# A list schedule of its own for the second layer's attention

## The chip, the cores and the metric

The kernel runs on one core of a Trainium2 chip. The metric is the device time of one execution in microseconds, the median over several runs. TensorE (PE in the profile; PEld is its loading of stationary operands) multiplies matrices and transposes; VectorE is DVE, ScalarE is ACT, GpSimd is POOL, and SyncE (SP) issues the DMA transfers. Each engine works through its own queue in order; semaphores between the queues make an instruction wait for another engine's.

## What is computed

A trunk of two layers over 512 tokens of width 1024. Layer 0 mixes tokens with a recurrence and a long convolution; layer 1 with 2-D neighbourhood attention, 16 heads of 64. Each layer has a gated feed-forward block and a gated per-layer input behind its mixer. All in float32. The part that the change touches:

```python
for i in range(DEPTH):
    ...
    else:
        z = rmsnorm(h, na_norm[j]) @ na_w_qkv[j]
        h = h + neighbourhood_attention(z, na_q_g[j], na_k_g[j], na_rpb[j]) @ na_w_out[j]
    h = h + conv_ffn(h, ffn_norm[i], ffn_w_up[i], ffn_conv_w[i], ffn_conv_b[i], ffn_w_down[i])
    h = h + per_layer_embedding(h, p[i], ple_norm[i], ple_w_gate[i], ple_w_proj[i])

def neighbourhood_attention(z, q_g, k_g, rpb):
    q = split(rmsnorm(z[..., :D].reshape(B, L, H, dh), q_g) * (dh ** -0.5))
    k = split(rmsnorm(z[..., D:2 * D].reshape(B, L, H, dh), k_g))
    v = split(z[..., 2 * D:])
    ...
    # per token: 8 rows x 16 columns of neighbours, scores plus a position bias, softmax, values
```

## The kernel before

The mixer of layer 0 is recorded into a `Plan`, a list scheduler: each instruction becomes a step with an estimated price, a group and the steps it depends on; a group has a priority; `schedule()` picks, engine by engine, the step of the highest rank among those that could start now or within AHEAD microseconds, and stays with one form of matmul until a run of RUN microseconds is full. `write()` (L590) then issues the steps in the order found, and `in_order` has the framework keep it. The price of a VectorE or ScalarE instruction is a formula: 0.15 or 0.16 us and a little over or under 1 ns for each element of a row.

Everything behind it (feed-forward 0, input 0, the attention `mixer1`, feed-forward 1, input 1) is written straight, and the framework orders it by the code and its dependencies. `mixer1` does this:

- The norm. For each of 8 blocks of the hidden state h, ScalarE scales and casts a high part xh and VectorE makes the low part xl; ScalarE squares (nsq) and GpSimd adds the squares up (nacc). `sums` multiplies nacc by a column of ones, four matmuls of 128x1, to get the sums over partitions; `rsqrt` makes rstd of them on VectorE (rv) and GpSimd.
- The projections. `gemm_tok` makes one of q, k, v for half of the heads: 4 chunks of weights, each two of the 8 blocks deep, come by DMA into wraw and are split into whi (cast on ScalarE) and wlo (VectorE), three slots each. A chunk feeds 24 matmuls of 128x512 (xh by whi, xh by wlo, xl by whi for 4 blocks of tokens), one PSUM bank "g" for each block of tokens. `evac` scales a bank by rstd on ScalarE; q and k then get a norm of their own (sq, ss, rs). The results of `sums` are therefore needed first when the first bank of q is complete. For v, six DMAs make a copy vb that is shifted by 64 tokens.
- `attend`, for each of 8 head pairs: q and k are transposed on TensorE (L1843) into PSUM "m" and split into qh, ql, kh, kl; four score tiles "s" of 6 matmuls each (64 rows of the array, one head) are made; VectorE adds the bias table and takes the maximum, ScalarE the exponential (sc), VectorE the division; the probabilities are transposed (L1892) and copied to pt on ScalarE (L1894); 32 small matmuls a pair multiply va or vb by pt into PSUM "m"; the result is split into oh (ScalarE, L641) and ol (VectorE, L633).
- The out projection: `gemm` with oh and ol, two halves of the depth by two groups of columns, added into h.

The code goes: projections of the first four pairs, their attention, projections of the other four, their attention, out projection. On TensorE the framework lets matmuls of a later gemm fill gaps between attention's steps, bank by bank as `gemm_tok` writes them. PSUM has four banks "g", two "s" and two "m". `sums` is called behind the second chunk of the first gemm (kc == 2).

The matmul helper is L627, elementwise VectorE and GpSimd operations of two tensors L633, ScalarE's functions L636, casts L641.

Of the kernel before, what the change touches and what calls it, by code (L numbers as in the profile page):

```python
# [22 lines left out]
KT = D // P  # L23
# [569 lines left out]
class Kern:  # L593
# [1131 lines left out]
    def gemm_tok(self, wname, g, xs, evac, then=None):  # L1725

        K, groups = WEIGHTS[wname]
        ps = [self.pg.tile([P, S], F32, name="g") for _ in range(4)]
        for kc in range(0, KT, 2):
            off = (g * KT + kc) * P * S  # L1730
            hi, lo = self.load_split(self.a[wname][off:off + 2 * P * S].rearrange("(p a) -> p a", p=P), 1024)
            for t in range(4):
                for kk in range(2):
                    c = slice(kk * S, (kk + 1) * S)
                    xh, xl = [x[:, t * P:(t + 1) * P] for x in xs(kc + kk)]
                    last = kc + kk == KT - 1
                    self.mm(ps[t], xh, hi[:, c], kc + kk == 0, False)
                    self.mm(ps[t], xh, lo[:, c], False, False)
                    self.mm(ps[t], xl, hi[:, c], False, last)
                if kc == KT - 2:  # L1740
                    evac(t, ps[t])
            if then is not None and kc == 2:
                then()

    def mixer1(self):

        nc, a = self.nc, self.a
        ident = self.cst("ident")
        by_col = lambda t: t.rearrange("p (r c) -> p c r", c=64)
        col = lambda t: t.rearrange("p (c r) -> p c r", r=8)  # L1750
        with ExitStack() as st:
            pa = self.pool(st, "pa", side="right")
            po = self.pool(st, "po", side="left")
            pss = self.pool(st, "pss", bufs=2, space=PSUM)
            xs, acc = [], None
            for k in range(KT):
                xh = self.px.tile([P, S], F32R, name=f"xh{k}")
                xl = self.px.tile([P, S], F32R, name=f"xl{k}")
                self.split(col(xh), col(xl), by_col(self.h[k]), scale=self.par("na_norm", k))
                xs.append((xh, xl))  # L1760
            for k in range(KT):
                sq = self.pn.tile([P, S], F32, name="nsq", bufs=2)
                self.act(col(sq), by_col(self.h[k]), AF.Square)
                if acc is None:
                    acc = sq
                else:
                    new = self.pn.tile([P, S], F32, name="nacc", bufs=2)
                    self.tt(new, acc, sq, ALU.add, nc.gpsimd)
                    acc = new
            rstd = pa.tile([P, 4], F32, name="rstd")  # L1770

            def sums():
                ps = self.pm.tile([P, 4], F32, name="m")
                for t in range(4):
                    self.mm(ps[:, t:t + 1], acc[:, t * P:(t + 1) * P], self.cst("one"))
                self.rsqrt(rstd, ps, 1.0 / D, EPS)

            oh = [(po.tile([P, S], F32R, name=f"oh{k}"), po.tile([P, S], F32R, name=f"ol{k}")) for k in range(KT)]
            for half in range(2):
                qk, vv = self.qkv(pa, half, lambda k: xs[k], rstd, sums if half == 0 else None)  # L1780
                for m in range(half * 4, half * 4 + 4):
                    self.attend(pa, pss, m, qk, vv, oh[m])
            for k0 in (0, 4):
                for g in range(2):
                    def evac(j, ps, g=g):
                        t = self.h[g * 4 + j]
                        self.tt(t, ps, t, ALU.add)
                    self.gemm("na_w_out", g, k0, k0 + 4, lambda k: oh[k], evac)
            for k in range(KT):
                self.dump(f"a_{k}", self.h[k])  # L1790

    def rsqrt(self, out, src, scale, eps):

# [2 lines left out]
        self.nc.vector.tensor_scalar(out=v[:, :n], in0=src, scalar1=scale, scalar2=eps, op0=ALU.mult, op1=ALU.add)  # L1796
        self.tt(out, v[:, :n], self.epsc[:, 4:4 + n], ALU.pow, self.nc.gpsimd)

    def qkv(self, pa, half, xs, rstd, then):


        nc = self.nc
        qk = [[pa.tile([P, S], F32, name=f"{n}{t}") for t in range(4)] for n in "qk"]
        va = pa.tile([P, 4, S], F32, name="va")
        vb = pa.tile([P, 3, S], F32, name="vb")

        def evac(t, ps, x):
            sc = rstd[:, t:t + 1]
            if x == 2:
                self.act(va[:, t], ps, AF.Copy, scale=sc)  # L1810
                return
            z = qk[x][t]
            self.act(z, ps, AF.Copy, scale=sc)
            sq = pa.tile([P, S], F32, name="sq", bufs=1)
            self.act(sq, z, AF.Square)
            ss = pa.tile([P, 8], F32, name="ss", bufs=2)
            nc.vector.tensor_reduce(out=ss, in_=sq.rearrange("p (h d) -> p h d", d=64), axis=AX.X, op=ALU.add)
            r = pa.tile([P, 8], F32, name="rs", bufs=2)
            self.rsqrt(r, ss, 1.0 / 64, EPS)
            zv = z.rearrange("p (h d) -> p h d", d=64)  # L1820
            self.tt(zv, zv, r.unsqueeze(2).to_broadcast([P, 8, 64]), ALU.mult)

        for x in range(3):
            self.gemm_tok("na_w_qkv", half * 3 + x, xs, lambda t, ps, x=x: evac(t, ps, x), then if x == 0 else None)
        for t in range(3):
            nc.sync.dma_start(out=vb[0:64, t], in_=va[64:128, t])
            nc.sync.dma_start(out=vb[64:128, t], in_=va[0:64, t + 1])
        return qk, (va, vb)
# [4 lines left out]
    def attend(self, pa, pss, m, qk, vv, o):  # L1833

        nc, ident = self.nc, self.cst("ident")
        c0 = m % 4 * P
        tab = pa.tile([P, 3, 512], F32, name="tab", bufs=2)
        nc.sync.dma_start(out=tab, in_=self.a["rpb"][m].rearrange("p (b x) -> p b x", b=3))
        q, k = [], []
        for x, dst in enumerate((q, k)):  # L1840
            ps = self.pm.tile([P, S], F32, name="m")
# [7 lines left out]
        scs = {}  # L1849
        for bp in range(2):  # L1850
            for hd in range(2):
                rows = slice(hd * 64, hd * 64 + 64)
                ps = pss.tile([P, 2, 256], F32, name="s")
                for bi in range(2):
                    b = bp * 2 + bi
                    w0 = self.WIN[b][0]
                    self.mm3(ps[:, bi], q[0][rows, b * P:(b + 1) * P], q[1][rows, b * P:(b + 1) * P],
                             k[0][rows, w0:w0 + 256], k[1][rows, w0:w0 + 256], True, True)
                sc = scs[bp, hd] = pa.tile([P, 2, 256], F32, name="sc", bufs=4)
                mx = pa.tile([P, 2], F32, name="mx", bufs=3)  # L1860
                sm = pa.tile([P, 2], F32, name="sm", bufs=3)
                for bi in range(2):
                    tb = tab[:, self.WIN[bp * 2 + bi][3], hd * 256:hd * 256 + 256]
                    nc.vector.tensor_tensor_reduce(out=sc[:, bi], in0=ps[:, bi], in1=tb, op0=ALU.add,
                                                   op1=ALU.max, scale=1.0, scalar=-3e38,
                                                   accum_out=mx[:, bi:bi + 1])
                nc.vector.tensor_scalar(out=mx, in0=mx, scalar1=-1.0, scalar2=None, op0=ALU.mult)
                for bi in range(2):
                    self.act(sc[:, bi], sc[:, bi], AF.Exp, bias=mx[:, bi:bi + 1],
                             accum_out=sm[:, bi:bi + 1])  # L1870
                nc.vector.reciprocal(out=sm, in_=sm)
                for bi in range(2):
                    nc.vector.tensor_scalar(out=sc[:, bi], in0=sc[:, bi], scalar1=sm[:, bi:bi + 1],
                                            scalar2=None, op0=ALU.mult)
        pts = {}
        pso = self.pm.tile([P, 4, P], F32, name="m")

# [69 lines left out]
```

## Time and profile before

| | us |
|---|---|
| runs | 1593.35, 1597.08, 1598.9 |
| median | 1597.08 |
| profiled execution, its own time | 1602.47 |
| span of its trace, first to last instruction | 1600.7 |
| PE busy | 1531.0 (96%) |
| DVE busy | 973.9 (61%) |
| ACT busy | 718.8 (45%) |
| POOL busy | 341.0 (21%) |

The mean granted clock of TensorE over the span is 0.974 of full speed. Matmuls are pipelined: one that is shown with 0.39 us starts about 0.23 us behind the one ahead, so the time that a row of matmuls takes is read from start to start. "Idle before" in brackets is how long the engine stood before the row's first instruction and what released it. The stage that is changed begins near 924 us and ends near 1189 us.

### The profile page before, as it was taken

To read this page: it belongs to the slowest core of one execution; us is meant where nothing else is said; L and a number is where in the kernel's file an instruction comes from. 1 tells how busy PE (TensorE), PEld (TensorE's weight loads), DVE (VectorE), ACT (ScalarE), POOL (GpSimd) and SP (SyncE) were. 2 spreads that over 40 slices of the span, in tenths; PEclk is the share of its full clock that TensorE was granted. 3 is DMA by queue.
4 is the path that set the end of the run, shared out by engine and by line. 5 is a ranking of instruction groups with operands and counts; after the bars stand their busy time and mean duration, and the time that the engine had idled before them with its cause. 6 is when DMAs were issued, how large, how long until landed. Compare 5 with 4: busy or idle time off the path is not lost.

```text
span 1600.7 us, 24569 instructions
## 1 busy us (share of the span) xinstructions
PE 1531.0 (96%) x9520; PEld 1219.6 (76%) x9520; DVE 973.9 (61%) x1618; ACT 718.8 (45%) x1210; POOL 341.0 (21%) x296
## 2 busy tenths in 40 slices
PE   7999999979797999999999999999999999999998
PEld 6766777657585888888888878777678888888886
DVE  4875677775654477534674664565666665366655
ACT  5636455535344344313443554564554443144332
POOL 4654554433554000000001332011030000000020
PEclk9999999979898999999999999999999999999999
DMA  7456464766354323223243234224122332222431
GB/s 235 122 126 193 139 195 130 226 206 203 128 184 135 100 96 102 92 96 102 92 128 122 86 112 124 94 81 130 61 66 79 105 105 93 93 88 97 160 104 66
DMA packets 114583, 195.97 MB, mean 122 GB/s; under 512 B 27537, under 2 KB 57105, under 8 KB 114466
## 3 DMA queue, kind: packets, MB, share of 16 engines
q1 hardware_dynamic: 114466, 194.40, 38.4%
q8 instruction: 75, 1.23, 0.3%
q14 instruction: 42, 0.34, 0.1%
HBM read 163.95 MB, written 28.84 MB: 120 GB/s over the span
## 4 chain that ended last, share of the span: by engine, by line
PE 84%; DVE 5%; DMA 4%; ACT 3%; SPq 2%; issue 1%; POOL 1%; POOLq 0%; DVEq 0%; ACTq 0%
PE g L627 61%; PE b L590 19%; DVE w L590 3%; SPq L590 2%; PE m L627 2%; PE s L627 1%; ACT w L590 1%; PE m L1892 1%; DMA wr<-in_mix_w_in 1%; POOL w L590 1%; DMA wr<-in_dft_f 0%; POOL nacc L633 0%; ACT oh L641 0%; DVE u L633 0%; DVE uv L590 0%
## 5 line engine op out<-in xcount | busy, mean ns | idle before, releaser
L633 DVE TENSOR_TENSOR wlo<-wraw,whi 128x1024 fp32r<-128x1024 f32 x180 | 227.8, 1267 | 322.5 <-ACT whi L641 317.7
L641 ACT CAST whi<-wraw 128x1024 fp32r<-128x1024 f32 x180 | 188.2, 1046 | 406.7 <-PE g L627 398.5
L627 PE MATMUL g<-xh,whi 128*128 128x512 f32 x832 | 326.8, 393 | 8.9 <-ACT whi L641 8.9
L627 PE MATMUL g<-xh,wlo 128*128 128x512 f32 x832 | 325.3, 391 | 1.0 <-DVE wlo L633 1.0
L627 PE MATMUL g<-xl,whi 128*128 128x512 f32 x832 | 324.9, 391 | 0.0
L627 PEld LDWEIGHTS g<-xh,whi 128*128 128x128 f32 x832 | 157.0, 189 | 43.0 <-ACT whi L641 9.3
L627 PEld LDWEIGHTS g<-xh,wlo 128*128 128x128 f32 x832 | 156.8, 188 | 34.7 <-DVE wlo L633 1.7
L627 PEld LDWEIGHTS g<-xl,whi 128*128 128x128 f32 x832 | 157.1, 189 | 32.3
L633 POOL TENSOR_TENSOR nacc<-nsq 128x512 f32<-128x512 f32 x5 | 8.8, 1767 | 760.5 <-PE g L627 639.6
L590 PE MATMUL b<-xh,wp 128*128 128x512 f32 x432 | 151.0, 423 | 10.5 <-ACT wp L590 10.2
L627 PE MATMUL g<-hh,whi 128*128 128x512 f32 x352 | 137.2, 390 | 0.0
L627 PE MATMUL g<-hl,whi 128*128 128x512 f32 x352 | 137.0, 389 | 0.0
L627 PE MATMUL g<-hh,wlo 128*128 128x512 f32 x352 | 136.9, 389 | 0.0
L630 DVE SCALAR_TENSOR_TENSOR c<-u,prm,c 128x511 f32<-128x511 f32 x176 | 126.3, 746 | 6.4 <-ACT c L636 5.9
L590 PEld LDWEIGHTS b<-xh,wp 128*128 128x128 f32 x432 | 83.2, 197 | 36.2 <-ACT wp L590 12.0
L636 ACT ACTIVATE c<-u,prm 128x512 f32<-128x512 f32 x88 | 70.3, 816 | 70.7 <-DVE u L633 70.7
L590 POOL TENSOR_TENSOR wp<-wr,wp 128x512 fp32r<-128x512 f32 x62 | 82.5, 1343 | 50.0 <-ACT wp L590 41.0
L590 POOL TENSOR_TENSOR w<-w 128x256 f32<-128x256 f32 (+2 forms) x69 | 75.7, 1115 | 74.2 <-ACT w L590 57.1
L590 PE MATMUL b<-xl,wp 128*128 128x512 f32 x216 | 89.0, 418 | 0.0
L633 DVE TENSOR_TENSOR u<-g,rstd 128x512 f32<-128x512 f32 x104 | 71.3, 686 | 11.6 <-PE g L627 10.8
L627 PE MATMUL g<-wlo,xh 128*128 128x512 f32 x192 | 77.2, 402 | 0.0
L627 PE MATMUL g<-whi,xh 128*128 128x512 f32 x192 | 77.1, 401 | 0.0
(181 smaller groups left out, 2601.4 us busy)
## 6 DMA issues: line engine op xcount, KB each, us to landing
wraw<-in_up SPq DMA_DIRECT2D x88, 512.0 KB, 3.5
wraw<-in_down SPq DMA_DIRECT2D x44, 512.0 KB, 3.5
wr<-in_mix_w_in SPq DMA_DIRECT2D x52, 256.0 KB, 3.7
wraw<-in_na_w_qkv SPq DMA_DIRECT2D x24, 512.0 KB, 3.5
x<-ch_d SPq DMA_DIRECT2D x16, 640.0 KB, 5.1
ch_d<-w SPq DMA_DIRECT2D x64, 128.0 KB, 2.3
wraw<-in_gate SPq DMA_DIRECT2D x16, 512.0 KB, 3.5
tab<-in_rpb SPq DMA_DIRECT2D x8, 768.0 KB, 4.2
```

The lines of the kernel that those rows point to most:

```text
L590: getattr(e, method)(*args, **kw)
L627: return self.nc.tensor.matmul(out, lhsT, rhs, start=start, stop=stop, skip_group_check=not group)
L630: return self.nc.vector.scalar_tensor_tensor(out=out, in0=in0, scalar=scalar, in1=in1, op0=op0, op1=op1)
L633: return (eng or self.nc.vector).tensor_tensor(out=out, in0=in0, in1=in1, op=op)
L636: return self.nc.scalar.activation(out=out, in_=in_, func=func, **kw)
L641: self.nc.scalar.copy(h, src)
L1892: nc.tensor.transpose(pst[:, i], sc[:, i // 2, (i % 2) * P:(i % 2 + 1) * P], ident)
```

## The change

The body of `mixer1` behind the norm's splits is recorded into a `Plan` of its own, with AHEAD 0.2 and RUN 1.5, and without the rule by which layer 0's plan prices a cold clock. Groups: the sums ("rms"), each projection gemm, and for each head pair its transposes of q and k, each score tile and its values; a table ORDER1 gives the priorities. The gemms are chained one behind the other, values of a pair behind those of the pair before, and the out projection's four gemms are at the end of the chain. The sums are called behind the third chunk (kc == 4) and not behind the second. What is computed, and by which instructions, is the same.

```diff
@@ gemm_tok
-            if then is not None and kc == 2:
-                then()
+            if then is not None and kc == 4:
+                self.nc.behind["rms"] = self.nc.group
+                self.part("rms", then)
@@ mixer1
+            start = len(nc.cur_bb.bb.instructions)
+            real, self.nc = nc, Plan(nc)
+            nc = plan = self.nc
+            plan.AHEAD, plan.RUN, plan.DRAG = self.ATTEND
+            plan.cold = False
...
+            dense = []
+
+            def gemm(group, what, *args):
+
+                if dense:
+                    plan.behind[group] = dense[-1]
+                dense.append(group)
+                self.part(group, what, *args)
...
-                qk, vv = self.qkv(pa, half, lambda k: xs[k], rstd, sums if half == 0 else None)
+                qk, vv = self.qkv(pa, half, lambda k: xs[k], rstd, gemm, sums if half == 0 else None)
...
-                    self.gemm("na_w_out", g, k0, k0 + 4, lambda k: oh[k], evac)
+                    gemm(("out", k0, g), self.gemm, "na_w_out", g, k0, k0 + 4, lambda k: oh[k], evac)
+            self.nc = real
+            plan.bias = {g: 1000.0 * self.order1(g) for g in plan.firsts}
+            plan.write(plan.schedule())
+            self.in_order(start)
+
+    ATTEND = 0.2, 1.5, 0.0
+    ORDER1 = dict(rms=90, qkv=50, qk=60, scores=70, values=80, out=40, vb=95)
+
+    def order1(self, group):
+        name, *n = group if isinstance(group, tuple) else (group,)
+        return self.ORDER1[name] - (n[0] if n else 0)
@@ attend
+        nc.group = "qk", m
+        nc.gates[nc.group] = [qk[0][0]]
...
+                nc.group = "scores", m, bp, hd
...
+        nc.group = "values", m
+        if m:
+            nc.behind[nc.group] = "values", m - 1
```

TensorE at the sums, before: the first gemm (q of the first four pairs), from the last matmuls of the second chunk to the first of the third. The names are out<-stationary or moving operands; xh_9003 and xh_9007 are blocks 2 and 3 of the input (second chunk), xh_9011 and xh_9015 blocks 4 and 5 (third chunk), xh_9019 block 6.

```order
L627 MATMUL g<-whi,xh_9007 128x512
L627 MATMUL g<-wlo,xh_9007 128x512
L627 MATMUL g<-whi,xl_9008 128x512
L627 MATMUL m<-con,nacc 128x1 x4
L627 MATMUL g<-whi,xh_9011 128x512
L627 MATMUL g<-wlo,xh_9011 128x512
L627 MATMUL g<-whi,xl_9012 128x512
```

And the same place in the new kernel, L590 being the line that writes the plan out.

```order
L590 MATMUL g<-wlo,xh_9015 128x512
L590 MATMUL g<-whi,xl_9016 128x512
L590 MATMUL m<-con,nacc 128x1 x4
L590 MATMUL g<-whi,xh_9019 128x512
L590 MATMUL g<-wlo,xh_9019 128x512
L590 MATMUL g<-whi,xh_9019 128x512
```

The four sums stand now between the third and the fourth chunk, and the dense matmuls go round the four banks two by two, where before one bank got all six of a chunk in a row.

TensorE amid the attention, before: scores of a pair of the first half, with matmuls of the second half's gemms between them.

```order
L627 MATMUL g<-wlo,xh_8995 128x512
L627 MATMUL g<-whi,xl_8996 128x512
L627 MATMUL g<-whi,xh_8999 128x512
L627 MATMUL g<-wlo,xh_8999 128x512
L627 MATMUL s<-kh,qh 128x256 x2
L627 MATMUL g<-whi,xl_9000 128x512
L627 MATMUL g<-whi,xh_8995 128x512
L627 MATMUL g<-wlo,xh_8995 128x512
L627 MATMUL s<-kl,qh 128x256
L627 MATMUL s<-kh,ql 128x256
```

The new kernel amid the attention of the first half (sc are the probabilities, transposed; pt with va and vb the values; q_9074 to q_9077 the blocks of q).

```order
L590 MATMUL s<-kh,ql 128x256
L590 MATMUL s<-kh,qh 128x256
L590 MATMUL m<-pt,va 64x128 x4
L590 MATMUL m<-pt,vb 64x128 x4
L590 MATMUL m<-con,sc 128x128 x4
L590 MATMUL g<-whi,xl_9004 128x512
L590 MATMUL g<-whi,xh_9007 128x512
L590 MATMUL g<-whi,xl_9004 128x512
L590 MATMUL g<-whi,xh_9007 128x512
L590 MATMUL m<-con,sc 128x128 x4
L590 MATMUL s<-kl,qh 128x256
L590 MATMUL s<-kh,ql 128x256
```

Scores stand there in longer runs, and some of them directly next to transposes and values; dense matmuls come in pieces between transposes.

ScalarE behind the v projection of the first half, before: va is the evacuation, qh and kh the splits of the transposed q and k, the casts of whi are weights of the next gemm.

```order
L636 ACTIVATE sq<-k_9081 128x512
L641 CAST whi<-wraw 128x1024 x3
L636 ACTIVATE va<-g,rstd 128x512 x4
L636 ACTIVATE qh<-m,epsc 128x512
L636 ACTIVATE kh<-m,prm 128x512
L641 CAST whi<-wraw 128x1024
L636 ACT_TABLE_LOAD
L636 ACTIVATE sc,sm<-sc,mx 128x256 x8
L1894 COPY pt<-m 128x512 x2
L641 CAST whi<-wraw 128x1024
```

And the same place in the new kernel.

```order
L590 ACTIVATE kh<-m,prm 128x512
L590 ACTIVATE sc,sm<-sc,mx 128x256 x2
L590 CAST whi<-wraw 128x1024
L590 ACTIVATE va<-g,rstd 128x512 x4
L590 CAST whi<-wraw 128x1024 x2
L590 COPY pt<-m 128x512
L590 CAST oh_9058<-m 128x64x8
L590 COPY pt<-m 128x512
L590 ACTIVATE sc,sm<-sc,mx 128x256
```

Two casts of weights stand directly behind the four evacuations of va, with pt, the cast of oh and exponentials behind them; attention's work of earlier pairs is spread around the evacuations, where before it began only behind them.

## Rows read from the trace of the kernel before

**Rows 1.** The chain that ended last: share of the span by engine.
```profile
PE 84%; DVE 5%; DMA 4%; ACT 3%; SPq 2%; issue 1%; POOL 1%; POOLq 0%; DVEq 0%; ACTq 0%
```

**Rows 2.** Stretches: length, busy us and (count) by engine, granted clock, DMA, GB/s.
```profile
924.50:938.50 14.00, 11.11 (x50) 8.85 (x49) 13.71 (x14) 12.34 (x13) 7.11 (x4) 1.00 0.20 69
938.50:945.40 6.90, 6.90 (x20) 5.80 (x21) 2.36 (x3) 0.00 (x0) 1.96 (x1) 0.51 0.74 285
...
1045.30:1051.50 6.20, 4.23 (x46) 3.17 (x45) 3.13 (x5) 4.60 (x7) 0.00 (x0) 1.00 0.45 161
```

**Rows 3.** Timeline of PE: start, us, line, operation, count, [idle before <- releaser].
```profile
924.57 0.39 PE L627 MATMUL g<-whi,xh 128*128 128x512 f32 x1
...
938.50 0.59 PE L627 MATMUL m<-con,nacc 128*128 128x1 f32 x2 [2.89 <-POOL nacc L633]
...
1188.56 0.39 PE L627 MATMUL g<-xh,whi 128*128 128x512 f32 x1
```

**Rows 4.** The chain in order of time: start, us, what; a plain dense stretch.
```profile
897.48 24.55 PE g L627 x108
```

**Rows 5.** Timeline of POOL and DVE at the norm.
```profile
936.51 1.93 POOL L633 TENSOR_TENSOR nacc<-nacc,nsq 128x512 f32<-128x512 f32 x1 [1.25 <-ACT nsq L636]
...
934.03 2.31 DVE L633 TENSOR_TENSOR wlo<-wraw,whi 128x1024 fp32r<-128x1024 f32 x1
```

**Rows 6.** Waits from 924 to 1189 us: us in total, times, longest.
```profile
PE m L1843 <- DVE ol L633: 4.1, 6, 1.6
```

**Rows 7.** Timeline of PE, transposes of k and the start of the last gemms.
```profile
1051.06 0.66 PE L1843 MATMUL m<-con,k 128*128 128x128 f32 x4 [1.60 <-DVE ol L633]
1051.47 0.48 PE L627 MATMUL g<-whi,xh 128*128 128x512 f32 x1
...
1174.58 0.73 PE L627 MATMUL g<-oh,whi 128*128 128x512 f32 x2 [1.11 <-ACT oh L641]
```

**Rows 8.** The tiles oh and ol: ns min/median/max, first and last start, forms.
```profile
L641 ACT CAST oh<-m x8: 1018/1072/1096, 1013.8 to 1173.5; 128x512 fp32r<-128x512 f32 x8
L633 DVE TENSOR_TENSOR ol<-m,oh x8: 1029/1042/1076, 1014.9 to 1174.6; 128x512 fp32r<-128x512 f32 x8
```

**Rows 9.** Timeline of PE, a run of scores between dense matmuls.
```profile
1040.17 0.50 PE L627 MATMUL g<-wlo,xh 128*128 128x512 f32 x1
1040.60 0.38 PE L627 MATMUL s<-kh,qh 64*128 64x256 f32 x1
1040.82 0.28 PE L627 MATMUL s<-kl,qh 64*128 64x256 f32 x1
...
1041.30 0.28 PE L627 MATMUL s<-kh,ql 64*128 64x256 f32 x1
1041.51 0.51 PE L627 MATMUL g<-whi,xl 128*128 128x512 f32 x1
1041.85 0.40 PE L627 MATMUL g<-whi,xh 128*128 128x512 f32 x1
```

**Rows 10.** Timeline of PE, values between dense matmuls and transposes.
```profile
1027.60 0.40 PE L627 MATMUL g<-wlo,xh 128*128 128x512 f32 x1
1027.92 0.66 PE L627 MATMUL m<-pt,va 128*64 128x128 f32 x8
1028.41 0.61 PE L627 MATMUL m<-pt,vb 128*64 128x128 f32 x8
1028.95 0.66 PE L1892 MATMUL m<-con,sc 128*128 128x128 f32 x4
1029.53 0.43 PE L627 MATMUL m<-pt,vb 128*64 128x128 f32 x2
1029.90 0.50 PE L627 MATMUL g<-whi,xl 128*128 128x512 f32 x1
```

**Rows 11.** Timeline of ACT, the evacuation of a bank of q.
```profile
949.78 0.69 ACT L636 ACTIVATE q<-g,rstd 128x512 f32<-128x512 f32 x1 [0.37 <-PE g L627]
```

**Rows 12.** The costliest groups: busy us, mean ns of one, idle before and its releaser.
```profile
L633 DVE TENSOR_TENSOR wlo<-wraw,whi 128x1024 fp32r<-128x1024 f32 x180 | 227.8, 1267 | 322.5 <-ACT whi L641 317.7
```

More of the change, by code (lines that the diff above doesn't have):

```diff
@@ L1787, in evac @@
                         self.tt(t, ps, t, ALU.add)
-                    self.gemm("na_w_out", g, k0, k0 + 4, lambda k: oh[k], evac)
-            for k in range(KT):
-                self.dump(f"a_{k}", self.h[k])
+                    gemm(("out", k0, g), self.gemm, "na_w_out", g, k0, k0 + 4, lambda k: oh[k], evac)
[8 more added lines that the diff above has]
+        return self.ORDER1[name] - (n[0] if n else 0)
     def rsqrt(self, out, src, scale, eps):
@@ L1797, in rsqrt, with qkv @@
         self.tt(out, v[:, :n], self.epsc[:, 4:4 + n], ALU.pow, self.nc.gpsimd)
-    def qkv(self, pa, half, xs, rstd, then):
+    def qkv(self, pa, half, xs, rstd, gemm, then):
         nc = self.nc
@@ L1823, in qkv @@
         for x in range(3):
-            self.gemm_tok("na_w_qkv", half * 3 + x, xs, lambda t, ps, x=x: evac(t, ps, x), then if x == 0 else None)
+            gemm(("qkv", half, x), self.gemm_tok, "na_w_qkv", half * 3 + x, xs, lambda t, ps, x=x: evac(t, ps, x),
+                 then if x == 0 else None)
+        nc.group = "vb", half
         for t in range(3):
```

## The prediction, made before the changed kernel had run

> **What bounds the kernel now.** I read the chain of waits first. TensorE carries 84% of it [rows 1], so a microsecond saved elsewhere counts only where TensorE waits for it. Next came TensorE's timeline, to find where the changed stage begins and ends: its first dense matmul (128x128 by 128x512, "g") starts at 924.57 us, and the first one of the following feed-forward block at 1188.56 [rows 3]. The stage takes 264.0 us on TensorE, and what the change does must show inside it, since everything before it is the same code and everything after it is moved as a block.
>
> What are the 264.0 us made of? The names and counts of the instructions come from the program; the pitch of each kind (start to start in a steady run) from rows. 768 dense matmuls: 24.55 us for 108 [rows 4], or 0.2273 each, 174.6 us. 192 transposes: four take 0.41 [rows 7], 19.8 us. 192 score matmuls ("s", 64 rows by 256): four steps take 0.48 [rows 9], 23.0 us. 256 value matmuls (pt with va or vb, 64 columns): eight take 0.49 [rows 10], 15.7 us. The sums 0.8. Waits: 2.89 for nacc [rows 3], 4.1 in six waits for ol [rows 6], 1.11 for oh [rows 7], 8.1 together. Half clock: after the wait for nacc the granted clock is 0.51 for 6.90 us, where it is 1.00 before [rows 2], that is 1.2 instead of 2.4 GHz, so (1 - 0.51) x 6.90 = 3.4 us are lost. These make 245.4 and leave 18.6 us.
>
> The 18.6 are the places where TensorE goes from one form of matmul to another. A run of scores between dense matmuls: from the dense one at 1040.17 to that at 1041.85 is 1.68 us [rows 9]; two dense and six scores at their pitch are 1.17; of the 0.51 left, 0.11 belongs to the run before it (the first dense matmul after a run is slow: 0.34 instead of 0.23 from 1041.51), so a round trip costs 0.40, and half of it, 0.20, for either way. For values [rows 10]: into them 0.32 - 0.23 = 0.09; out of them, two values and the way take 0.37, so 0.25, and with the slow first dense matmul 0.35; a visit from dense and back is 0.44; a trip to four transposes and back 0.17 + 0.05, about 0.2. Before, the order has 29 runs of scores and 23 of values, 12 of them entered from dense and 11 from transposes: 29 x 0.40 + 12 x 0.44 + 11 x 0.2 = 19.1 us. That is close to the 18.6 left over, so the prices stand, scaled by 0.97.
>
> **The change, part by part.** No instruction is added or dropped; only the order on each engine changes.
>
> (A) The sums move from behind the second chunk of weights to behind the third. Now they are reached at 935.6 and wait until nacc is done (936.51 + 1.93 = 938.44 [rows 5]). Behind the third chunk TensorE would be there at 924.57 + 72 x 0.2273 = 940.9, so the 2.89 are gone, and with them, I take it, the fall of the clock that followed (3.4). In its place TensorE comes to the third chunk at 935.5 and needs that chunk's low half with its second matmul, at 935.7; VectorE ends it at 934.03 + 2.31 = 936.34 [rows 5]: a new wait of up to 0.7. The order puts the low half of the fourth chunk and that of the next gemm ahead of the reading of the sums, and rstd behind that; the first bank of q is complete only after some 90 matmuls, around 945, and these 4 us cover it. Without that cover each microsecond of lateness would show as one. A = 2.9 + 3.4 - 0.7 = 5.6 us gained. Bounds: 2.2 if the clock falls all the same, 6.3 if the low half comes in time.
>
> (B) The waits for ol (the transposes of k stand behind the split of the head pair before, since they need its PSUM buffer "m") and for oh at the end. In the new order dense matmuls or other work stand there: the out projection's second half keeps well over a hundred dense matmuls behind the last values. 4.1 + 1.1 = 5.2 us. I add no clock to this: in the stretch with the longest of these waits (1.60, [rows 7]) TensorE is busy 4.23 of 6.20 us and the granted clock stays 1.00 [rows 2].
>
> (C) Fewer changes of form. After, there are 17 runs of scores and 19 of values. Scores meet dense matmuls on 21 of their 34 sides, 21 x 0.20 = 4.2; values are entered from dense 16 times at 0.09 = 1.4, left to dense 6 times at 0.35 = 2.1, left to transposes 12 times at 0.1 = 1.2; together 8.9. On 13 sides scores now stand directly next to transposes or values. No row of before shows that. The nearest rows are 0 (transposes next to dense, where no gap is left [rows 7]) and 0.25 (from values to dense [rows 10]); I take 0.20, the side of a score run next to dense, since transposes have the same form as dense matmuls: 2.6. After 11.5 x 0.97 = 11.2, so 18.6 - 11.2 = 7.4 gained. With the bounds 0 and 0.25 for the 13 sides it is 9.9 or 6.8.
>
> The Trainium skill, "TensorEngine Tiling (Array Packing)", section Key Properties, says that changing the tiling mode, and not merely the tile, drains TensorE. By it each of the 13 sides pays, and the sum stays at about 2.6 us; by the cheap end of the rows it would be 0. The rows agree that a price hangs on the mode, since transposes next to dense matmuls have none; they disagree that it is one price, with 0.09 into values and 0.35 out of them.
>
> (D) What the list schedule loses. Its order is right only if its prices are. The cast of oh takes 1.07 and ol 1.04 [rows 8], where its formula (0.16 or 0.15 plus 512 elements at 0.86 or 1.06 ns) gives 0.60 and 0.69: 0.47 + 0.35 = 0.8 us too early for each of 8 head pairs, 6.6 in all if TensorE waits for each. And it deals the dense matmuls round the four PSUM banks, two to each, so that all four end within 6 matmuls of each other; 9 times a next gemm comes 7 to 13 matmuls behind, 1.6 to 3.0 us, in which ScalarE must free the banks at 0.69 each [rows 11]: one late bank each is 9 x 0.69 = 6.2. So D lies between 0 and 12.8 us lost. I take 4: the rows it is nearest to are the waits of before, 4.1 in six for the same split, and in the new order most values are followed by dense work that needs neither.
>
> The sum: 5.6 + 5.2 + 7.4 - 4 = 14.2 us. The profiled execution took 1602.5 us and would take 1588.3; the median of the three runs, 1597.1, becomes 1582.9; I say 1583.0. The feed-forward block that follows is dense work of the same order, and starts earlier by as much.
>
> **Rivals.** First, the banks: every hand-over waits for one evacuation and every head pair for its split, D = 12.8 in place of 4. For it: ScalarE also has the exponentials and casts of weights in that stretch. Against it: the evacuations of before are as many and as long, and none of TensorE's waits there is put down to one. 1583.0 + 8.8 = 1591.8, but with about half of it, the likelier case, 1587.
>
> Second, the order buys almost nothing: the tile framework's order before already had dense matmuls in the gaps, what waits on TensorE goes by ScalarE's and VectorE's chain of softmax and casts, and this is as long as it was. Then B and C are given back as waits, and A remains at 2.2 to 5.6: 1591.5 to 1594.9, about 1593.
>
> Third, slower: casts of weights at the head of ScalarE's and VectorE's queues. Each chunk must wait for a slot of three, that is until TensorE is through an earlier chunk; the new order puts two casts directly behind the evacuation of v, with pt and the exponentials queued behind them, and the low halves likewise on VectorE. If TensorE then has nothing that needs neither, it stands while two low halves are made, 2 x 1.27 = 2.5 us [rows 12], a wait as long as that for nacc, which cost 3.4 of clock behind it: 5.9 a place. To be slower than 1597.1 by 4.8 it takes (14.2 + 4.8)/5.9, four places of the six gemms that stand amid attention; four give 1583 + 24 = 1607. Against it: at the two places where such casts stand the new order leaves TensorE some 30 dense matmuls, 6.8 us.
>
> **How the numbers follow.** Forecast with D from 0 to 8: 0.68, at 1577 to 1587. First rival at its full price: 0.11 (1588 to 1592). Second: 0.13, of which about a third falls below 1592.3. Third: 0.08. What a measurement can tell from no change is 0.3%, or 4.8 us. So faster than 1592.3: 0.68 + 0.11 + 0.04 = 0.83; same: 0.09; slower: 0.08. The low end: D at 0 and the 13 sides at 0 give 14.2 + 4 + 2.5 = 20.7, so 1576.4, and with the 3 us by which the runs differ 1574. The high end, 1592, takes in D at its full 12.8. Above it lies some 0.17, below 1574 a few hundredths.
>
> **What would show it.** A: no wait for nacc, the sums at about 941, and a granted clock of 1.00 from 938 to 946; wrong if the clock is at half anywhere near, or if q's evacuation waits for rstd. B: no wait for ol ahead of the transposes of k, and no 1.1 us for oh at the end. C: about 11 us left after the same subtraction over the stage; a start-to-start time from the last score to a transpose near 0.3 for the price I took, near 0.12 for none. D: the waits of TensorE in the stage add up to about 4 us, in pieces below 1; pieces of 0.7 on g for q, k or va speak for the first rival, pieces over 2 us on pt or sc with a half clock behind them for the third. The stage as a whole should be about 250 us; at 260 or more the forecast is wrong.

## The result

The changed kernel takes 1584.95 us (median of 8 runs, 1581.58 to 1590.96), the kernel before 1596.46 us (median of 8, 1593.35 to 1599.71). The ratio is 0.9924, with a 95% interval from 0.9906 to 0.9941: 0.76% or about 12 us faster. The prediction said 1583.0, with a range of 1574 to 1592.

The gain is where it was looked for. The stage, from its first dense matmul to the first one of feed-forward 1, took 264.0 us on TensorE [rows 3]. In the trace of the changed kernel it lasts from 922.14 to 1174.23 us, 252.1, so it is 11.9 us shorter. From there to the end of the span it is 412.2 us, where it was 412.1.

### The profile page after: what moved, and what is told of

Its sections match the earlier page's. It is cut to its first block, busy times and chain, and to the rows that moved or that the text cites. A ratio compares the mean times of both kernels' runs of the same rounds, so it can differ in the third digit from the quotient of the medians.

```text
span 1586.4 us, 24570 instructions
## 1 busy us (share of the span) xinstructions
PE 1516.3 (96%) x9520; PEld 1213.7 (77%) x9520; DVE 979.9 (62%) x1618; ACT 717.7 (45%) x1210; POOL 342.6 (22%) x296
## 4 chain that ended last, share of the span: by engine, by line
PE 82%; DMA 5%; DVE 5%; issue 2%; ACT 2%; POOL 2%; SPq 2%; DVEq 0%; POOLq 0%; ACTq 0%
PE g L627 50%; PE b L590 16%; PE g L590 11%; DVE w L590 3%; PE m L590 3%; SPq L590 2%; DMA wr<-in_mix_w_in 2%; PE s L590 1%; POOL w L590 1%; DVE u L633 1%; ACT w L590 1%; DMA wr<-in_dft_f 1%; POOL wp L590 1%; DMA uv<-vt_d 0%; DVE uv L590 0%
## 5 line engine op out<-in xcount | busy, mean ns | idle before, releaser
L633 DVE TENSOR_TENSOR wlo<-wraw,whi 128x1024 fp32r<-128x1024 f32 x148 | 187.1, 1265 | 294.1 <-ACT whi L641 289.6
L641 ACT CAST whi<-wraw 128x1024 fp32r<-128x1024 f32 x148 | 154.8, 1046 | 354.9 <-PE g L627 346.9
L590 PE MATMUL b<-xh,wp 128*128 128x512 f32 x432 | 147.9, 415 | 11.7 <-ACT wp L590 10.6
L590 PEld LDWEIGHTS b<-xh,wp 128*128 128x128 f32 x432 | 81.0, 192 | 36.9 <-ACT wp L590 12.3
L590 POOL TENSOR_TENSOR wp<-wr,wp 128x512 fp32r<-128x512 f32 x62 | 82.2, 1336 | 47.7 <-ACT wp L590 41.9
L590 POOL TENSOR_TENSOR w<-w 128x256 f32<-128x256 f32 (+2 forms) x69 | 75.9, 1118 | 71.8 <-ACT w L590 55.5
L590 PE MATMUL b<-xl,wp 128*128 128x512 f32 x216 | 87.5, 411 | 0.0
L590 DVE TENSOR_TENSOR w<-w 128x512 f32<-128x512 f32 (+16 forms) x116 | 68.8, 610 | 17.9 <-DMA w<-nd 10.8
L627 PEld LDWEIGHTS g<-hh,whi 128*128 128x128 f32 x352 | 66.1, 188 | 14.2 <-DVE u L633 0.5
```

The source lines that it names most:

```text
L590: getattr(e, method)(*args, **kw)
L627: return self.nc.tensor.matmul(out, lhsT, rhs, start=start, stop=stop, skip_group_check=not group)
L633: return (eng or self.nc.vector).tensor_tensor(out=out, in0=in0, in1=in1, op=op)
L641: self.nc.scalar.copy(h, src)
```

## The profile after

The timeline of TensorE in the changed kernel: the entry into the stage, with the first matmul on the fourth PSUM bank; the sums; and the first matmul behind the stage. Columns: start us, us, line, operation, count, [idle before <- releaser].

```profile
922.14 0.39 PE L590 MATMUL g<-whi,xh 128*128 128x512 f32 x1
...
925.34 0.50 PE L590 MATMUL g<-whi,xh 128*128 128x512 f32 x1 [1.67 <-DVE u L633]
...
940.44 0.95 PE L590 MATMUL m<-con,nacc 128*128 128x1 f32 x8
941.24 0.49 PE L590 MATMUL g<-whi,xh 128*128 128x512 f32 x1
...
1174.23 0.39 PE L627 MATMUL g<-xh,whi 128*128 128x512 f32 x1
```

The row of the sums answers to that at 938.50 in [rows 3]: no idle time stands before it now. The windows of the same kernel (length, busy us by engine, granted clock, DMA share, GB/s) show what followed:

```profile
922.10:936.00 13.90, 12.23 (x54) 9.78 (x54) 13.69 (x14) 12.14 (x13) 7.18 (x4) 1.00 0.07 18
936.00:946.00 10.00, 10.00 (x50) 8.38 (x49) 3.70 (x4) 1.56 (x3) 2.16 (x2) 1.00 0.59 197
922.10:1174.20 252.10, 248.04 (x1417) 197.42 (x1417) 156.70 (x391) 140.34 (x276) 44.27 (x24) 1.00 0.30 98
```

The granted clock is 1.00 through the whole stage, where [rows 2] had 0.51 for 6.90 us. And all that TensorE waited for in the stage (total, times, longest):

```profile
PE s L590 <- DVE mx L590: 1.8, 5, 0.5
PE g L590 <- DVE u L633: 1.7, 1, 1.7
PE m L590 <- DVE sm L590: 0.2, 1, 0.2
```

The waits for ol [rows 6], for oh [rows 7] and for nacc [rows 3] are gone, and other ones have come: for VectorE to read a bank that the gate of the block before had filled (u), and for its reading of a score tile (mx). This view leaves out pieces under 0.15 us; three of them, 0.3 us together, are counted in the table below.

Where the time of the stage goes, by kind of work on TensorE. Each figure is the sum, over the runs of one kind, of the time from the run's first start to the first start of the next kind, less the idle time shown there; so the price of a change of form is split between its two sides. All the kernels that ran stand here, in us, named as in the next section:

| kernel | stage | waits | dense | sums | transposes | scores | values |
|---|---|---|---|---|---|---|---|
| before | 264.0 | 8.5 | 190.7 | 1.7 | 20.3 | 23.4 | 19.4 |
| after | 252.1 | 4.0 | 184.3 | 0.8 | 20.1 | 25.4 | 17.5 |
| sums_third | 258.5 | 6.2 | 188.4 | 0.8 | 20.3 | 23.4 | 19.4 |
| plan_second | 253.2 | 4.9 | 184.4 | 0.9 | 20.1 | 25.4 | 17.5 |
| banks | 253.7 | 4.3 | 184.4 | 0.8 | 20.8 | 25.5 | 17.8 |
| run0 | 257.0 | 5.4 | 184.9 | 0.8 | 21.3 | 26.7 | 17.8 |
| before_inter | 270.6 | 13.4 | 189.8 | 1.7 | 22.1 | 23.1 | 20.6 |
| inter | 242.1 | 3.7 | 183.6 | 0.8 | 21.4 | 14.6 | 18.0 |
| inter_price | 241.4 | 4.0 | 184.0 | 0.8 | 20.4 | 14.5 | 17.7 |
| inter_ah5 | 247.2 | 9.0 | 183.6 | 0.8 | 21.6 | 14.8 | 17.4 |

One column goes the wrong way in the changed kernel: its scores cost 25.4 us, 2.0 more than before, although they stand in 17 runs in place of 29.

## The experiments

Small effects are read from the stage in the trace. The part ahead of it, whose code is the same in all kernels, ended between 910.8 and 927.5 us in the profiled executions, which is more than most of these edits do; ratios are therefore given beside the stage. Each stage is that of one traced execution, but kernels with the same order there agree in the table to 0.1 us: before and sums_third in transposes, scores and values, after and plan_second in everything but waits and sums.

In two runs the stage and the medians tell different sizes. The medians of plan_second (1590.48) and banks (1590.10) stand 5 us above the changed kernel's 1584.95, their stages only 1.1 and 1.6 us. The granted clock over a whole execution averages 0.9786 and 0.9789 in their runs and 0.9804 in those of the changed kernel, which is some 2 to 3 us of 1590. Where the executions without a trace lost it is not on record; in the traced ones it was not in the stage.

### sums_third: the sums alone

```diff
-            if then is not None and kc == 2:
+            if then is not None and kc == 4:
                 then()
```

> The kernel before, with one edit: the sums stand behind the third chunk of weights and not behind the second; no list schedule. My sum (part A): the wait of 2.89 us for nacc goes, and with it the half clock behind it (3.4 us), against up to 0.7 for the low half of the third chunk: the stage falls from 264.0 to about 258.4 us and the median by 5.6. Rival: the clock falls for another reason and stays at half for some 6.9 us: then only 2.2 to 2.9 us are gained. If the change of order of the list schedule is what counts and the sums were covered anyway: 0.

Ratio 0.9970 (0.9949 to 0.9991), stage 258.5 us: 5.5 less than before, against 5.6 expected. TensorE's waits in the stage, and the windows where the clock had been at half, in this kernel's time:

```profile
PE m L1843 <- DVE ol L633: 4.1, 6, 1.6
PE g L627 <- ACT oh L641: 1.1, 1, 1.1
PE g L627 <- DVE wlo L633: 0.6, 1, 0.6
PE m L627 <- ACT pt L1894: 0.4, 1, 0.4
```

```profile
934.00:940.00 6.00, 6.00 (x32) 5.09 (x31) 3.29 (x4) 1.05 (x1) 1.77 (x1) 1.00 0.74 275
940.00:947.00 7.00, 7.00 (x33) 5.79 (x32) 2.32 (x5) 4.28 (x8) 2.93 (x3) 1.00 0.35 118
```

The wait for nacc and the half clock go together, and 0.6 us for the low half of the third chunk comes in, all as part A had it. A second kernel that keeps the sums and the order of before around them, before_inter below, has the wait (2.9 us) and the half clock again:

```profile
931.70:938.60 6.90, 6.86 (x20) 5.80 (x21) 2.40 (x3) 0.00 (x0) 1.96 (x1) 0.51 0.76 300
```

In sums_third dense matmuls and sums lose 2.3 + 0.9 = 3.2 us in the table: that is what the half clock had cost, estimated at 3.4. The rival by which the clock falls anyway is out.

### plan_second: the list schedule with the sums where they were

```diff
-            if then is not None and kc == 4:
+            if then is not None and kc == 2:
                 self.nc.behind["rms"] = self.nc.group
```

> The changed kernel, with the sums back behind the second chunk. Its second chunk would end near 934.7 us and nacc at 936.1, so TensorE should stand about 1.4 us there. If a wait of this size leaves the clock alone, as the waits of 1.6 and 1.1 us of the kernel before did, the stage goes from 252.1 to 253.5 us. Rival: the place, and not the length of the wait, is what brings the clock to half: then 1.4 + 3.4 = 4.8 us are lost, 256.9.

Ratio 0.9954 (0.9941 to 0.9968), stage 253.2 us, 1.1 above the changed kernel. The timeline at the sums, and the window behind them:

```profile
935.67 1.05 PE L590 MATMUL m<-con,nacc 128*128 128x1 f32 x8 [0.92 <-POOL nacc L633]
```

```profile
935.60:942.50 6.90, 6.83 (x34) 5.81 (x35) 2.44 (x3) 0.38 (x2) 1.99 (x2) 1.00 0.57 192
```

A wait of 0.92 us, and the clock stays at 1.00. So by the stage moving the sums is worth 5.5 us without the list schedule and 1.1 with it. The two edits are not additive: under the list schedule TensorE comes to the sums 13.0 us behind its first matmul of the stage, where before it came after 11.0; 1.67 of that is the wait at the entry, and nacc is nearly ready. Undone alone, this part of the change would be put at 1.1 us by the trace; of the 5.5 us between the medians, some 3 go with the granted clock, and what is left beyond the 1.1 stays open.

### banks: the wait at the entry

The plan deals its first matmuls round the four PSUM banks, two to each, and does not know that the fourth is still being read. Here it is told so.

```diff
+            plan.held = dict(g=[0.0, 0.0, 0.0, 9.8])
...
-            return slots.setdefault(key(t), [0.0] * self.bufs(self.tiles[t]))
+            return slots.setdefault(key(t), list(self.held.get(t.split('_')[0], [0.0] * self.bufs(self.tiles[t]))))
```

(The 9.8 is in the plan's own time, in which I put the first matmul some 6 us behind the plan's start, hence 9.8 for 3.4; no trace shows the plan's own times.)

> The changed kernel, with the plan told that the fourth PSUM bank g comes free 3.4 us after the others at its start. Theory: the wait of 1.67 us at the start of the stage (for VectorE's reading of the gate's last bank) is there because the plan deals the first matmuls round all four banks at once; with 14 matmuls on the other three banks ahead it goes: 1.7 us less, 250.4. Rival: TensorE meets the next thing that is late (the low half of the second chunk, or the splits of the last blocks of h) and nothing is gained.

Ratio 0.9947 (0.9927 to 0.9968), stage 253.7 us, 1.6 longer than the changed kernel's. TensorE's waits:

```profile
PE s L591 <- DVE mx L591: 2.2, 5, 0.5
PE g L591 <- DVE wlo L591: 1.3, 1, 1.3
PE m L591 <- DVE q L591: 0.2, 1, 0.2
PE g L591 <- ACT q L591: 0.2, 1, 0.2
```

The 1.67 us are gone and 1.3 us for the low half of a chunk have come: the rival's case. In the changed kernel VectorE is busy 13.69 of the first 13.90 us of the stage (the windows above), so TensorE meets it at one place or the next. Waits make 0.3 of the 1.6. Transposes make 0.7 and values 0.3, in another order, dense matmuls and scores the little that is left; I take all this for a by-effect of rescheduling.

### run0: more changes of form

```diff
-    ATTEND = 0.2, 1.5, 0.0
+    ATTEND = 0.2, 0.0, 0.0
```

> The changed kernel with RUN at 0: the list schedule no longer stays with one form of matmul for 1.5 us. Its order has 22 runs of scores in place of 17, 20 of values in place of 19, 52 of dense in place of 51, 40 of transposes in place of 38. If a change of form costs the 0.1 on either side that the traces show, some 9 more changes are 0.9 us and the stage goes from 252.1 to about 253. But where a break of a run brings the other head's matmuls next to it, the scores get cheaper: six of one head in a row take 0.72, pairs of two heads half of that; that rival gives up to 3 us less, 249 to 251.

Ratio 0.9962 (0.9937 to 0.9986), stage 257.0 us: 4.9 more than the changed kernel, where I had expected 0.9 more and the rival up to 3 less. Waits make 1.3 of it; dense 0.7, transposes 1.2, scores 1.3 and values 0.4 the other 3.5, for 9 more runs of one form: 0.4 each, where I had put 0.1. A part of that is in the rows: the first matmul behind a change is slow as well (0.34 in place of 0.23 [rows 9]), which makes 0.2. The rest is not the price of a change alone: TensorE goes from transposes to scores at 10 places in place of 5, three fewer pairs of scores start together (see the next run), and one more run of values is split. The six-score runs are still of one head, so nothing got cheaper. Under this list schedule, staying with one form for 1.5 us is worth 4.9 of the 11.9 us of the stage.

### inter: the scores of two heads alternately

Why are long runs of scores dear? The timeline of the changed kernel, a run of 12 between a dense matmul and transposes:

```profile
986.41 0.38 PE L590 MATMUL s<-kh,qh 64*128 64x256 f32 x1
986.63 0.28 PE L590 MATMUL s<-kl,qh 64*128 64x256 f32 x1
986.75 0.27 PE L590 MATMUL s<-kh,ql 64*128 64x256 f32 x1
...
987.81 0.28 PE L590 MATMUL s<-kh,ql 64*128 64x256 f32 x1
988.01 0.66 PE L590 MATMUL m<-con,sc 128*128 128x128 f32 x4
988.43 0.48 PE L590 MATMUL g<-whi,xh 128*128 128x512 f32 x1
988.74 0.40 PE L590 MATMUL g<-wlo,xh 128*128 128x512 f32 x1
```

and of the kernel before, within a run of 10 that took 1.01 us:

```profile
1018.94 0.29 PE L627 MATMUL s<-kh,ql 64*128 64x256 f32 x1
1018.95 0.38 PE L627 MATMUL s<-kl,qh 64*128 64x256 f32 x1
1019.07 0.28 PE L627 MATMUL s<-kh,qh 64*128 64x256 f32 x1
1019.17 0.28 PE L627 MATMUL s<-kh,ql 64*128 64x256 f32 x1
1019.18 0.28 PE L627 MATMUL s<-kl,qh 64*128 64x256 f32 x1
```

In this run of the new order each starts 0.12 behind the last or later; before, some start 0.01 behind it. I take those to be of the two heads, which the code puts on rows 0 to 63 and 64 to 127 of the array, running at the same time. The framework's order happened to mix the heads; the list schedule has a group for each head, and takes one head's six in a row. Over the stage, 41 of the 192 scores start within 0.05 us of the one ahead in the kernel before, and 15 in the changed one. The edit puts both heads into one group, alternately:

```diff
         for bp in range(2):
-            for hd in range(2):
-                nc.group = "scores", m, bp, hd
-                rows = slice(hd * 64, hd * 64 + 64)
-                ps = pss.tile([P, 2, 256], F32, name="s")
-                for bi in range(2):
-                    b = bp * 2 + bi
-                    w0 = self.WIN[b][0]
-                    self.mm3(ps[:, bi], q[0][rows, b * P:(b + 1) * P], q[1][rows, b * P:(b + 1) * P],
-                             k[0][rows, w0:w0 + 256], k[1][rows, w0:w0 + 256], True, True)
+            nc.group = "scores", m, bp
+            pair = [pss.tile([P, 2, 256], F32, name="s") for _ in range(2)]
+            for bi in range(2):
+                b = bp * 2 + bi
+                w0 = self.WIN[b][0]
+                for x, y in ((0, 0), (0, 1), (1, 0)):
+                    for hd in range(2):
+                        rows = slice(hd * 64, hd * 64 + 64)
+                        self.mm(pair[hd][:, bi], q[x][rows, b * P:(b + 1) * P], k[y][rows, w0:w0 + 256],
+                                x + y == 0, x == 1)
+            for hd in range(2):
+                ps = pair[hd]
```

> The changed kernel, with the score matmuls of the two heads of a pair taken alternately (one group for both heads), so that neighbours stand on different halves of the array's rows. Theory: the list schedule's long runs of one head are dear because their matmuls all stand on the same 64 rows and run one at a time; 12 of one head take 1.61 us, 12 mixed ones of the kernel before took 1.25. 16 x 0.36 = 5.8 us less, or more if all pairs run at once; score time 25.4 to 19.6 us or below. Rival: both PSUM buffers s must now be free at the same time, so TensorE waits for VectorE's reading before each of 16 pairs, 0.5 us each as in the three such waits now: 8 us lost, 2 us slower in all.

1574.88 us, ratio 0.9868 (0.9834 to 0.9901), stage 242.1 us: 10.0 less than the changed kernel, where at least 5.8 was expected. A run of 12:

```profile
980.67 0.39 PE L590 MATMUL s<-kh,qh 64*128 64x256 f32 x2
980.89 0.28 PE L590 MATMUL s<-kl,qh 64*128 64x256 f32 x2
981.01 0.28 PE L590 MATMUL s<-kh,ql 64*128 64x256 f32 x2
981.12 0.28 PE L590 MATMUL s<-kh,qh 64*128 64x256 f32 x2
981.24 0.28 PE L590 MATMUL s<-kl,qh 64*128 64x256 f32 x2
981.36 0.28 PE L590 MATMUL s<-kh,ql 64*128 64x256 f32 x2
981.57 0.66 PE L590 MATMUL m<-con,sc 128*128 128x128 f32 x4
```

Twelve take 0.90 us here, as long as six of one head [rows 9], so the second head is free. 94 of the 192 scores now start within 0.05 us of the one ahead. TensorE's busy time with s in the stage (the windows of that tile alone; length, PE, PEld, DVE) in the kernel before, the changed one and this one:

```profile
924.50:1188.50 264.00, 25.44 (x192) 19.55 (x192) 25.10 (x64) 0.99 0.29 93
```

```profile
922.10:1174.20 252.10, 26.62 (x192) 22.12 (x192) 25.12 (x64) 1.00 0.30 98
```

```profile
914.40:1156.50 242.10, 15.69 (x192) 12.42 (x192) 24.55 (x64) 1.00 0.31 103
```

The rival fell: TensorE waits 3.7 us in this stage, less than in the changed kernel, and none of it ahead of a score.

### before_inter: the same without a list schedule

The edit of inter without its groups, in the kernel before.

> The kernel before, without the list schedule and with the sums behind the second chunk, but with the score matmuls of a pair's two heads written alternately. Theory: neighbours on different halves of the array's rows run at the same time whoever orders them, so the 31 runs of scores cost 192 x 0.06 + 31 x 0.2 = 17.7 us in place of 23.4: the stage goes from 264.0 to about 258 us. Rival: the framework takes one head's matmuls first wherever one buffer s is free before the other, and the alternation is lost, or TensorE waits for both buffers: within 2 us of 264.

1602.12 us, ratio 1.0033 (1.0017 to 1.0050): slower. The stage is 270.6 us, 6.6 longer, more than either case had. The framework breaks the twelve up between dense matmuls: runs of ten fall from 1.02 to 0.79 us, but the runs of two (0.32) and six (0.90) are as they were, and the scores come to 23.1 in place of 23.4. And TensorE waits 13.4 us in place of 8.5. These waits are new:

```profile
PE m L1895 <- DVE sc L1876: 2.1, 3, 1.3
PE m L1895 <- ACT pt L1897: 2.0, 1, 2.0
PE s L627 <- DVE mx L1867: 1.0, 1, 1.0
```

Most of them are for the softmax. That they come from both buffers s being taken at once is likely, but no run shows it alone. A second stretch at half clock (last section) costs some 1.4 us more. So in these runs the alternation paid where the order kept the twelve together, and not where the framework broke them up.

### inter_price and inter_ah5: can the plan do better?

```diff
                 t = 0.004 + n * 0.000447
+                if rows <= 64 and n == 256:
+                    t = 0.06
```

> The kernel with the two heads' scores taken alternately, and the plan's price of such a matmul at 0.06 us in place of 0.118, about what that run showed (0.076 with the ends of the runs). Theory: a right price takes away what waits are left from scores that end earlier than planned: up to 1 us less than 242.1. Rival: the order it finds has as many changes of form (123 against 122) and nothing is gained: within 0.7 us.

1575.50 us, ratio 0.9860 (0.9834 to 0.9885), stage 241.4 us: 0.7 less than inter, at the bound between both theories, and the medians tell no difference. It waits 4.0 us, 1.3 of it for a DMA (vb<-va), which inter does not.

```diff
-    ATTEND = 0.2, 1.5, 0.0
+    ATTEND = 0.5, 1.5, 0.0
```

> The kernel with the two heads' scores taken alternately, and AHEAD 0.5 in place of 0.2: the plan may let an engine stand up to 0.5 us for a step of higher rank. Its order has 115 runs of one form in place of 122. By the changes alone 7 x 0.15 = 1 us less than 242.1. Rival: the waits that it plans, of up to 0.5 each, are real, and cost more than that: 243 to 246.

1579.16 us, ratio 0.9877 (0.9841 to 0.9914), stage 247.2 us: 5.1 longer than inter, and more than the rival gave. The changes of form are fewer and save 0.2 us, but TensorE waits 9.0 us in place of 3.7, in pieces of up to 1.3 for ol and 0.9 for sc. A reason may be that with waits planned so tight, work that the plan prices too low (the split into oh and ol) ends late; no run tests this.

With the heads alternated under the list schedule, all three kernels beat the changed one in their medians; inter and inter_price are 1.3 and 1.4% faster than the kernel before.

## Why the prediction came out as it did

**The bound.** Right: the gain is the stage's, and what comes behind moves as a block (412.1 and 412.2 us).

**A, the sums: 5.6 expected.** In the changed kernel the wait of 2.9 and the half clock of 3.2 us are gone, and the 0.7 for the low half of the third chunk did not come, since TensorE is later there by 1.67 us; 6.1. Alone, in sums_third, the step gave 5.5 with every piece close to what was summed up. What the step didn't say is that its worth depends on the entry: with the list schedule around it, it is 1.1 in the traced stage.

**B, attention's waits: 5.2 expected.** The waits for ol and oh are gone, and so is one of 0.4 us for pt that the sum left out: 5.6.

**C, fewer changes of form: 7.4 expected, 4.2 measured.** This is the term that was mis-sized. Dense matmuls gave 4.1 (188.4 without the half clock, to 184.3), values 1.9, transposes 0.2, but scores took 2.0 more. The step priced each score at 0.12 us, "start to start in a steady run", from a run of six of one head [rows 9], and gave all the saving to the number of runs. That pitch is one of one head alone; where the heads mix it is half, and the new order unmixes them. The count of scores that start together falls from 41 to 15: 26 at 0.12 are 3.1 us, nearly all of the 3.2 that are missing, and inter, which brings the count to 94, takes the scores from 25.4 to 14.6 us. The sign that the prediction named, about 11 us left after the same subtraction over the stage, comes out at 252.1 - 233.9 - 4.0 = 14.2 (233.9 being its 245.4 without waits and half clock).

Two more sizes in this step were off, and about cancel. A wait inside a run of scores costs more than its idle time, since the run starts slowly again:

```profile
1016.33 0.28 PE L590 MATMUL s<-kh,ql 64*128 64x256 f32 x1
1016.76 0.39 PE L590 MATMUL s<-kh,qh 64*128 64x256 f32 x1 [0.15 <-DVE mx L590]
1016.99 0.28 PE L590 MATMUL s<-kl,qh 64*128 64x256 f32 x1
```

From 1016.33 to 1016.99 are 0.66 us; without 0.15 of idle time and two steps of 0.12 it is 0.27, and the five waits for mx make 1.3 us of it, booked under scores. The rest of the step came out better than summed up by about as much, and no run takes that apart. For the 13 sides of scores next to transposes or values, the prediction named as a sign about 0.3 us from the last score to a transpose for its price of 0.20, and 0.12 for none. It is 0.20 (987.81 to 988.01), so on the way out of scores the price is nearer 0.08. And it read transposes next to dense matmuls as free [rows 7]. They are not, though both use the whole array: the first dense matmul behind them takes 0.31 to the next (988.43 to 988.74) and not 0.23.

The Trainium skill has the rule, on the page that the prediction itself drew on: "TensorEngine Tiling (Array Packing)", section Key Properties, says right behind the drain at a change of mode that tiles operate independently and can load and multiply in parallel. The traces agree with it: twelve matmuls alternating between two tiles of 64 rows take 0.90 us (inter), twelve on one take 1.60 (986.41 to 988.01 in the changed kernel). The prediction weighed the one rule and not the other.

**D, the plan's own waits: 4 taken, 4.0 measured,** but not by the working given. There is no wait for oh or ol, and none for an evacuation of g within the stage. They are 1.7 at the entry, 1.8 for VectorE's reading of scores, 0.2 for the softmax and 0.3 in small pieces. The entry is the nearest to what was written: the dealing round four banks asks for the fourth bank after 6 matmuls, where the kernel before came to it after 18, and it still belongs to the block ahead, which the sum had not looked at. That piece of 1.67 is also over the "pieces below 1" that the prediction named as its sign. The size is right by luck.

**The sum.** 6.1 + 5.6 + 4.2 - 4.0 = 11.9 us, against 14.2. **The rivals.** No bank hand-over inside the stage was waited for, only the one at the entry; at no place in the changed kernel did a cast of weights hold TensorE; and B and C were not given back as waits. A kernel where planned waits do take over is inter_ah5.

## What to carry to other kernels

Price a matmul on part of the array together with its neighbours in the queue: on another part of it the neighbour is free, on the same part it is not, and a scheduler with one group for each head undoes such pairs unseen. Before costing a step by a pitch, look whether the starts in other runs of the same kind are as far apart. When two edits both take slack from one place, such as an entry where VectorE is full, undoing one of them tells little about what it is worth without the other.

## What the runs showed of the hardware that was not expected

Where the clock falls. In before_inter a second stretch at half clock stands behind a wait of 1.97 us for pt:

```profile
1040.30 0.66 PE L1895 MATMUL m<-con,sc 128*128 128x128 f32 x4 [1.97 <-ACT pt L1897]
```

```profile
1033.00:1040.40 7.40, 5.06 (x28) 3.29 (x27) 6.50 (x31) 5.72 (x19) 0.00 (x0) 1.00 0.27 87
1040.40:1043.80 3.40, 3.40 (x25) 2.57 (x25) 0.23 (x1) 0.91 (x2) 0.00 (x0) 0.59 0.54 198
```

The granted clock is 0.59 over those 3.40 us, so mostly at 1.2 GHz, after waits of 0.4 and 2.0 us amid transposes. Waits of 1.67 at the entry (changed kernel), 1.60 [rows 7] and 0.92 (plan_second) were not followed by it. Splitting a run of values is dear, too: 16 in one piece take 1.02 us, but 14 and 2 apart 1.02 and 0.36. The kernel before has seven such splits and the changed one three, which is 1.4 of the 1.9 us that its values gained.
